# Narrow part of a matmul gradient transposed, with new phase lengths and shared rounding

## The chip, the cores and the metric

The kernel runs on one core of one Trainium2 chip. The metric is the device time of one execution in microseconds (us). Engines are named as in the profile: PE is the matmul engine, PEld its weight loads, DVE the vector engine, ACT the scalar engine, POOL and SP the engines that here mostly issue DMAs. L123 is line 123 of the kernel that the view belongs to, so line numbers differ between kernels. The granted clock is the share of PE's full clock that the profile says PE was given.

## The reference

```python
# input: 16 x 512 x 1024 float32, grad_output: 16 x 512 x 768 float32
grad_weight = np.einsum('bmk,bmn->kn', input, grad_output)     # 1024 x 768
```

Batch and rows together are 8192 rows, taken in 64 **slices** of 128 rows. Each slice gives X (128 x 1024) and G (128 x 768), and the result is the sum over all slices of X transposed times G.

## The kernel before: the parts that matter

All 1024 x 768 outputs would take twelve PSUM tiles of 128x512 float32 (**banks**), and the kernel's pool holds eight, so the slices are worked in **phases**. In each phase, the wide part (512 of the 768 columns of G) takes eight banks, one for each 128 rows of the output. Then the narrow part (256 columns) follows. At the end of a pass a bank is added to an accumulator in SBUF.

```python
PHASES = [2, 4, 6, 10, 14, 18, 10]
...
if not last:                                   # wide: slice by slice, 8 banks
    for i, s in enumerate(slices[:-1]):
        for k in range(KS):
            nc.tensor.matmul(banks[k], xblk[s](k), gwide[s], start=(i == 0), stop=False)
for k in range(KS):
    if last:                                   # last phase: one bank after the other,
        bank = psum.tile([P, NA], f32, name="bank")     # each over all its slices
        for i, s in enumerate(slices[:-1]):
            nc.tensor.matmul(bank, xblk[s](k), gwide[s], start=(i == 0), stop=False)
    ...
# narrow_group: X block as weights, 256 columns of G stream
for i, s in enumerate(slices):
    nc.tensor.matmul(dst, xblk[s](k), gnarrow[s][:, c0:c1], ...)
```

Slices 0 and 1 come as float32 and are rounded to bf16 on DVE and ACT. All others come through a POOL queue that rounds on the way. Eleven warm-up matmuls run while the first data load.

## Time and profile before

| | before |
|---|---|
| time, median (range) | 177.36 us (177.28 to 177.38) |
| span of the profiled execution | 175.6 us |
| PE busy | 171.2 us, 97% of the span |
| DMA engines | about full until 144 us |
| first real matmul, start of the last matmul | 5.43 us, 172.57 us |

The gap of 1.76 us between time and span lies outside the profile. "Busy" does not mean "at its peak" for PE, because matmuls are pipelined and overlap in the record. The distance between two starts is the measure, and it comes from the chain of waits in order of time. The groups by shape give counts and the length of one instruction. Columns: line, engine, operation, output and inputs, count, then busy us and mean ns of one, then idle us before them.

```profile
L144 PE MATMUL bank<-gt,xt 128*128 128x512 bf16 x367 | 81.5, 379 | 0.5
L123 PE MATMUL bank<-gt,xt 128*128 128x256 bf16 x486 | 54.0, 273 | 0.0
L123 PEld LDWEIGHTS <-xt 128*128 128x128 bf16 x506 | 48.7, 98 | 6.8
```

A matmul of 512 columns is on record for 379 ns, though they start 215.8 ns apart. Weight loads of 98 ns lie beside matmuls. Some matmul records are missing (367 of 376 in the first line), so idle time below is computed from the first and last start and the instruction count, not by summing gaps.

### The profile page before, as it was taken

How to read it: one execution, taken by the hardware profiler on the slowest of the kernel's cores; microseconds unless marked ns; L12 is line 12 of the kernel's file. 1: busy time of each engine (PE TensorE's matmuls, PEld its weight loads, DVE VectorE, ACT ScalarE, POOL GpSimd, SP SyncE). 2: the span in 40 equal slices, each digit the busy share in tenths (PEclk: the TensorE clock that was granted, in tenths of full speed). 3: DMA queues.
4: the chain of work that ended last, by engine and by line, in shares of the span. 5: the costliest groups of instructions: out<-in, count | busy, mean ns of one | idle time of the engine just before them, and what ended most of it. 6: DMA issues, size and time to landing. Idle time of an engine off the chain costs nothing.

```text
span 175.6 us, 2484 instructions
## 1 busy us (share of the span) xinstructions
PE 171.2 (97%) x1033; PEld 101.7 (58%) x1045; DVE 54.2 (31%) x93; ACT 8.0 (5%) x15; POOL 66.6 (38%) x129
## 2 busy tenths in 40 slices
PE   8999999999999999999999999999999999999993
PEld 3364844764446864444488744444458886444783
DVE  0662990970008530000381300000047112333332
ACT  2451300000000000000000000000000000000000
POOL 7444434444444444444444444444364100000000
PEclk9999999999999999999999999999999999999999
DMA  5999999999999999999999999999999990333432
GB/s 196 288 207 209 208 208 209 209 208 209 207 208 207 209 209 210 208 209 207 209 207 209 208 210 208 209 206 208 208 210 208 209 169 0 119 119 119 144 126 92
DMA packets 21595, 33.45 MB, mean 190 GB/s; under 512 B 2385, under 2 KB 12497, under 8 KB 21585
## 3 DMA queue, kind: packets, MB, share of 16 engines
q0 software_dynamic: 18128, 28.58, 89.1%
q1 hardware_dynamic: 3168, 3.67, 6.0%
q10 hardware_dynamic: 288, 1.05, 1.5%
q8 instruction: 8, 0.13, 0.3%
q14 instruction: 3, 0.02, 0.0%
HBM read 58.72 MB, written 3.15 MB: 352 GB/s over the span
## 4 chain that ended last, share of the span: by engine, by line
PE 81%; DMA 15%; POOL 1%; issue 1%; DVE 0%; POOLq 0%
PE bank L144 38%; PE bank L123 29%; DMA xt<-in_input_dram 15%; PE bank L149 9%; PE bank L153 5%; POOL gt L101 1%; POOL gn L88 0%; POOL xt L102 0%; DVE acc L119 0%; POOLq L199 0%
## 5 line engine op out<-in xcount | busy, mean ns | idle before, releaser
L144 PE MATMUL bank<-gt,xt 128*128 128x512 bf16 x367 | 81.5, 379 | 0.5
L119 DVE TENSOR_TENSOR acc<-bank,acc 128x512 f32<-128x512 f32 (+2 forms) x69 | 41.8, 646 | 107.6 <-PE bank L153 82.1
L144 PEld LDWEIGHTS <-xt 128*128 128x128 bf16 x376 | 36.8, 98 | 43.3 <-DMA xt<-in_input_dram 0.2
L123 PE MATMUL bank<-gt,xt 128*128 128x256 bf16 (+1 forms) x506 | 55.2, 270 | 0.0
L123 PEld LDWEIGHTS <-xt 128*128 128x128 bf16 x506 | 48.7, 98 | 6.8
L102 POOL DMA_DIRECT2D xt<-in_input_dram x62 | 33.0, 532 | 38.7 <-DMA xt<-in_input_dram 33.8
L101 POOL DMA_DIRECT2D gt<-in_grad_output_dram x62 | 32.9, 531 | 30.7 <-DMA gt<-in_grad_output_dram 28.8
L149 PE MATMUL bank<-gt,xt 128*128 128x512 bf16 x70 | 16.7, 379 | 0.1
L153 PE MATMUL bank<-gt,xt 128*128 128x512 bf16 x47 | 12.4, 379 | 0.2 <-DMA xt<-in_input_dram 0.2
L149 PEld LDWEIGHTS <-xt 128*128 128x128 bf16 x72 | 7.1, 98 | 8.3
L153 PEld LDWEIGHTS <-xt 128*128 128x128 bf16 x48 | 4.5, 97 | 6.4 <-DMA xt<-in_input_dram 1.2
L113 DVE COPY acc<-bank 128x512 f32<-128x512 f32 x10 | 6.2, 683 | 5.7 <-PE bank L153 5.7
L68 PE MATMUL bank<-const-bfloat16-1.0 128*128 128x512 bf16 x11 | 4.9, 630 | 0.8 <-PEq L199 0.8
L115 ACT COPY acc<-bank 128x512 f32<-128x512 f32 x10 | 5.3, 597 | 6.1 <-PE bank L153 5.7
L119 DVE TENSOR_TENSOR acc<-acc,acc 128x512 f32<-128x512 f32 x8 | 5.0, 680 | 0.0
L68 PEld LDWEIGHTS <-const-bfloat16-1.0 128*128 128x128 bf16 x11 | 1.5, 143 | 3.2 <-issue 3.2
L73 DVE CAST g<-gf 128x512 bf16<-128x512 f32 x2 | 0.9, 426 | 5.6 <-DMA gf<-in_grad_output_dram 5.6
L144 PE MATMUL bank<-g,x 128*128 128x512 bf16 x8 | 2.1, 415 | 0.0
L123 PE MATMUL bank<-gn,x 128*128 128x256 bf16 x16 | 1.9, 273 | 0.0
L153 PE MATMUL bank<-g,x 128*128 128x512 bf16 x8 | 1.9, 379 | 0.0
L123 PEld LDWEIGHTS <-x 128*128 128x128 bf16 x16 | 1.6, 98 | 0.4
L144 PEld LDWEIGHTS <-x 128*128 128x128 bf16 x8 | 0.8, 108 | 1.6 <-DVE x L79 0.7
(9 smaller groups left out, 5.7 us busy)
## 6 DMA issues: line engine op xcount, KB each, us to landing
xt<-in_input_dram POOLq DMA_DIRECT2D x62, 256.0 KB, 8.5
gt<-in_grad_output_dram POOLq DMA_DIRECT2D x62, 192.0 KB, 8.5
out_dram<-acc SPq DMA_DIRECT2D x13, 128.0 KB, 1.7
out_dram<-acc SPq DMA_DIRECT2D x5, 256.0 KB, 2.0
xf<-in_input_dram ACTq DMA_DIRECT2D x2, 512.0 KB, 4.9
gf<-in_grad_output_dram SPq DMA_DIRECT2D x2, 256.0 KB, 4.6
gn<-in_grad_output_dram POOLq DMA_DIRECT2D x1, 128.0 KB, 6.1
out_dram<-acc SPq DMA_DIRECT2D x2, 64.0 KB, 1.6
```

Source lines behind the costliest of these rows:

```text
L68: nc.tensor.matmul(wps, ones, ones_wide, start=(i == 0), stop=(i == WARMUP - 1))
L73: nc.vector.tensor_copy(out=gt, in_=gf[s])
L101: nc.gpsimd.dma_start(out=gt, in_=G[s * P : (s + 1) * P, :])
L102: nc.gpsimd.dma_start(out=xt, in_=X[s * P : (s + 1) * P, :])
L113: nc.vector.tensor_copy(out=dst, in_=src)
L115: nc.scalar.copy(out=dst, in_=src)
L119: nc.vector.tensor_add(out=dst, in0=src, in1=dst)
L123: nc.tensor.matmul(dst, xblk[s](k), gnarrow[s][:, c0:c1], start=(i == 0), stop=(i == len(slices) - 1),)
L144: nc.tensor.matmul(banks[k], xblk[s](k), gwide[s], start=(i == 0), stop=False)
L149: nc.tensor.matmul(bank, xblk[s](k), gwide[s], start=(i == 0), stop=False)
L153: nc.tensor.matmul(bank, xblk[s](k), gwide[s], start=False, stop=True)
```

## The change

The intent: stream X in pieces of 512 columns for the narrow part too, with 128 columns of G as weights. The narrow result then comes out transposed. At the end DVE turns it in 32x32 blocks, and the store puts the blocks in place. Taking even and odd columns of G as two weight sets lets neighbouring columns meet again in the turned tile, so that stored runs are 64 floats and not 32. The phases become shorter at the start, and the last one is longer. The last phase also changes its order: it begins with the narrow pass, slice by slice, and the wide blocks follow one by one. Its last output block is cut in three, so that the last add and store are 128 columns wide, as they were before. The core of the diff (cut):

```diff
-PHASES = [2, 4, 6, 10, 14, 18, 10]
+PHASES = [2, 3, 4, 5, 8, 10, 18, 14]
...
-        nc.vector.tensor_copy(out=gt, in_=gf[s])          # G whole on DVE
-        ... quarters of X on DVE and ACT in turn
+        for dst, src in ((gt, gf[s]), (xt, xf[s])):       # both in 256-column pieces
+            for i in range(0, dst.shape[1], 2 * QX):
+                nc.vector.tensor_copy(out=dst[:, i : i + QX], in_=src[:, i : i + QX])
+                nc.scalar.copy(out=dst[:, i + QX : i + 2 * QX], in_=src[:, i + QX : i + 2 * QX])
...
+            t, h = groups[j]                              # t: even or odd, h: half of X
             nc.tensor.matmul(
-                dst, xblk[s](k), gnarrow[s][:, c0:c1], ...
+                banks[j],
+                gnarrow[s].rearrange("p (r t) -> p t r", t=NT)[:, t],
+                xs[s][:, h * NA : (h + 1) * NA], ...
...
+    def add_and_turn(t, h, dst, src):
+        add_out(dst, src)
+        nc.vector.transpose(out=turned[:, h * hb : (h + 1) * hb, :, t],
+                            in_=dst.rearrange("p (b r) -> p b r", r=SQ))
...
+        # last phase: narrow first, slice by slice; then the wide blocks one by one
+        narrow_pass(slices, add_and_turn, streamed=True)
+        store_turned()                                    # four stores, 256-byte runs
         for k in range(KS):
+            pieces = [(0, NA)] if k < KS - 1 else [(0, 256), (256, 384), (384, NA)]
```

More of the change, by code (lines that the diff above doesn't have):

```diff
@@ L35 @@
     NB = N - NA
+    NT = NB // P
+    KH = K // NA
     assert sum(PHASES) == S and PHASES[0] == HW
@@ L45 @@
     psum = ctx.enter_context(tc.tile_pool(name="psum", bufs=8, space=bass.MemoryType.PSUM))
-    acc = accp.tile([P, KS, N], f32, name="acc")
-    acc1 = accp.tile([P, KS, NA], f32, name="acc1")
-    xblk = [None] * S
+    acc = accp.tile([P, KS, NA], f32, name="acc")
+    acct = accp.tile([P, NT, K], f32, name="acct")
+    spare = accp.tile([P, KS, NA], f32, name="spare")
+    xs = [None] * S
     gwide = [None] * S
@@ L72 @@
         gt = head.tile([P, NA], bf16, name=f"g{s}")
-        nc.vector.tensor_copy(out=gt, in_=gf[s])
-        xq = []
-        for i in range(K // QX):
-            xt = head.tile([P, QX], bf16, name=f"x{s}_{i}")
-            src = xf[s][:, i * QX : (i + 1) * QX]
-            if i % 2 == 0:
-                nc.vector.tensor_copy(out=xt, in_=src)
-            else:
-                nc.scalar.copy(out=xt, in_=src)
-            xq.append(xt)
-        xblk[s] = lambda k, xq=xq: xq[k // 2][:, (k % 2) * P : (k % 2 + 1) * P]
+        xt = head.tile([P, K], bf16, name=f"x{s}")
+        for dst, src in ((gt, gf[s]), (xt, xf[s])):
+            for i in range(0, dst.shape[1], 2 * QX):
+                nc.vector.tensor_copy(out=dst[:, i : i + QX], in_=src[:, i : i + QX])
+                nc.scalar.copy(out=dst[:, i + QX : i + 2 * QX], in_=src[:, i + QX : i + 2 * QX])
+        xs[s] = xt
         gwide[s] = gt[:, :]
@@ L102, in load_upto @@
             nc.gpsimd.dma_start(out=xt, in_=X[s * P : (s + 1) * P, :])
-            xblk[s] = lambda k, xt=xt: xt[:, k * P : (k + 1) * P]
+            xs[s] = xt
             gwide[s] = gt[:, 0:NA]
@@ L119, in add_out, with wide_mm @@
         nc.vector.tensor_add(out=dst, in0=src, in1=dst)
-    def narrow_group(dst, k, slices, c0, c1):
-        for i, s in enumerate(slices):
-            nc.tensor.matmul(
-                dst,
-                xblk[s](k),
-                gnarrow[s][:, c0:c1],
-                start=(i == 0),
-                stop=(i == len(slices) - 1),
+    SQ = 32
+    def wide_mm(bank, k, s, start, stop, c0=0, c1=NA):
+        nc.tensor.matmul(
+            bank, xs[s][:, k * P : (k + 1) * P], gwide[s][:, c0:c1], start=start, stop=stop
+        )
@@ new lines, in wide_pass, with narrow_pass, mm @@
+    def wide_pass(slices, evacuate):
+        banks = [psum.tile([P, NA], f32, name="bank") for _ in range(KS)]
+        for s in slices:
+            for k in range(KS):
+                wide_mm(banks[k], k, s, s == slices[0], s == slices[-1])
+                if s == slices[-1]:
+                    evacuate(k, banks[k])
+    def narrow_pass(slices, evacuate, streamed):
+        groups = [(t, h) for t in range(NT) for h in range(KH)]
+        banks = [psum.tile([P, NA], f32, name="bank") for _ in groups]
+        def mm(j, s):
+            t, h = groups[j]
+            nc.tensor.matmul(
+                banks[j],
+                gnarrow[s].rearrange("p (r t) -> p t r", t=NT)[:, t],
+                xs[s][:, h * NA : (h + 1) * NA],
+                start=(s == slices[0]),
+                stop=(s == slices[-1]),
+            )
+        if streamed:
+            for s in slices[:-1]:
+                for j in range(len(groups)):
+                    mm(j, s)
+        for j, (t, h) in enumerate(groups):
+            for s in slices[-1:] if streamed else slices:
+                mm(j, s)
+            evacuate(t, h, acct[:, t, h * NA : (h + 1) * NA], banks[j])
@@ new lines, with store_turned @@
+    turned = spare.rearrange("p a b -> p (a b)")[:, 0 : NT * K].rearrange(
+        "p (b r t) -> p b r t", t=NT, r=SQ
+    )
+    def add_and_turn(t, h, dst, src):
+        add_out(dst, src)
+        hb = NA // SQ
+        nc.vector.transpose(
+            out=turned[:, h * hb : (h + 1) * hb, :, t],
+            in_=dst.rearrange("p (b r) -> p b r", r=SQ),
+        )
+    def store_turned():
+        rows = out.rearrange("(b r) n -> r b n", r=SQ)
+        for a in range(P // SQ):
+            c = NA + a * NT * SQ
+            nc.scalar.dma_start(
+                out=rows[:, :, c : c + NT * SQ],
+                in_=turned[a * SQ : (a + 1) * SQ].rearrange("p b r t -> p b (r t)"),
@@ L140, with evacuate_wide @@
         if not last:
-            banks = [psum.tile([P, NA], f32, name="bank") for _ in range(KS)]
-            for i, s in enumerate(slices[:-1]):
+            def evacuate_wide(k, bank):
+                if ph == 0:
+                    copy_out(acc[:, k, :], bank)
+                elif ph == 1:
+                    copy_out(spare[:, k, :], bank)
+                else:
+                    add_out(acc[:, k, :], bank)
+            wide_pass(slices, evacuate_wide)
+            narrow_pass(
+                slices,
+                lambda t, h, dst, src: (copy_out if ph == 0 else add_out)(dst, src),
+                streamed=False,
+            )
@@ L143 @@
+            if ph == 1:
                 for k in range(KS):
-                    nc.tensor.matmul(banks[k], xblk[s](k), gwide[s], start=(i == 0), stop=False)
+                    add_out(acc[:, k, :], spare[:, k, :])
+            continue
+        narrow_pass(slices, add_and_turn, streamed=True)
+        store_turned()
         for k in range(KS):
-            if last:
-                bank = psum.tile([P, NA], f32, name="bank")
-                for i, s in enumerate(slices[:-1]):
-                    nc.tensor.matmul(bank, xblk[s](k), gwide[s], start=(i == 0), stop=False)
-            else:
-                bank = banks[k]
@@ L152 @@
-            s = slices[-1]
-            nc.tensor.matmul(bank, xblk[s](k), gwide[s], start=False, stop=True)
-            if ph == 0:
-                copy_out(acc[:, k, 0:NA], bank)
-            elif ph == 1:
-                copy_out(acc1[:, k, :], bank)
-            else:
-                add_out(acc[:, k, 0:NA], bank)
-            if last:
-                W = NB if k < 3 else NA
-                for c in range(0, NA, W):
-                    nc.sync.dma_start(out=OUT[:, k, c : c + W], in_=acc[:, k, c : c + W])
@@ L166 @@
-        if not last:
-            for k in range(0, KS, 2):
-                bank = psum.tile([P, 2, NB], f32, name="bank")
-                for j in range(2):
-                    narrow_group(bank[:, j, :], k + j, slices, 0, NB)
-                dst = acc[:, k : k + 2, NA:N]
-                (copy_out if ph == 0 else add_out)(dst, bank)
-        else:
-            for k in range(KS):
-                pieces = [(0, NB)] if k < KS - 1 else [(0, NB // 2), (NB // 2, NB)]
-                for c0, c1 in pieces:
-                    bank = psum.tile([P, NA], f32, name="bank")
-                    narrow_group(bank[:, 0 : c1 - c0], k, slices, c0, c1)
-                    dst = acc[:, k, NA + c0 : NA + c1]
-                    add_out(dst, bank[:, 0 : c1 - c0])
-                    nc.sync.dma_start(out=OUT[:, k, NA + c0 : NA + c1], in_=dst)
@@ L182 @@
-        if ph == 1:
-            for k in range(KS):
-                add_out(acc[:, k, 0:NA], acc1[:, k, :])
+            pieces = [(0, NA)] if k < KS - 1 else [(0, 256), (256, 384), (384, NA)]
+            for c0, c1 in pieces:
+                bank = psum.tile([P, NA], f32, name="bank")[:, 0 : c1 - c0]
+                for s in slices:
+                    wide_mm(bank, k, s, s == slices[0], s == slices[-1], c0, c1)
+                add_out(acc[:, k, c0:c1], bank)
+                W = NB if k < 6 else c1 - c0
+                for c in range(c0, c1, W):
+                    nc.sync.dma_start(out=OUT[:, k, c : c + W], in_=acc[:, k, c : c + W])
```

## The prediction

> **What bounds the kernel now.** I read the page first: busy shares, the 40 slices, the chain that ended last.
>
> ```profile
> PE 171.2 (97%) x1033; PEld 101.7 (58%) x1045; DVE 54.2 (31%) x93; ACT 8.0 (5%) x15; POOL 66.6 (38%) x129
> ...
> PE   8999999999999999999999999999999999999993
> ...
> PEclk9999999999999999999999999999999999999999
> DMA  5999999999999999999999999999999990333432
> ...
> PE 81%; DMA 15%; POOL 1%; issue 1%; DVE 0%; POOLq 0%
> ```
>
> The matmul engine is busy from end to end at the full clock. The DMA engines are nearly as full until about 144 us, so both limits lie close together. Busy does not mean at its peak, so I took the matmul pace from the chain in order of time:
>
> ```profile
> 20.89 9.49 DMA xt<-in_input_dram
> 30.38 0.05 issue
> 30.42 1.90 PE bank L153 x8
> 32.32 5.24 PE bank L123 x48
> ...
> 39.56 10.74 PE bank L144 x49
> 50.30 0.05 issue
> ...
> 131.04 15.72 PE bank L123 x144
> ...
> 164.03 8.77 PE bank L123 x90
> 172.80 0.02 issue
> 172.83 0.29 DVE acc L119
> ```
>
> From 30.42 us on, the chain is matmuls without a gap. The 49 matmuls of 512 columns and the 0.05 us "issue" piece are 50 issues in 10.79 us: 0.2158 us each. The 256-column ones take 15.72/144 = 0.1092 us. The last 90 are 70 of 256 columns (7.64 us) and 20 of 128 columns, which leaves 1.13/20 = 0.056 us each. Before 30.42 us the chain runs over loads. The timeline shows the first real matmul at 5.43 us, where the last warm-up matmul also ends. From 5.43 to 30.42 are 24.99 us, and the work in them is 88 x 0.2158 + 48 x 0.1092 = 24.23 us. So all the idle time of the matmul engine is **0.76 us**: about 0.24 us at the first matmuls (8 take 2.13 us where the next 8 take 1.89) and about 0.52 us waiting for slices 5 and 11 (the weight loads of L153 wait for input tiles twice, 1.2 us in all, part of it behind running matmuls).
>
> The end: last add over at 173.12 us, span 175.6 us, so 2.5 us for the last store. Time per run is 177.36, thus 1.76 us more than the span; I keep that constant.
>
> **What the Trainium skill says.** "TensorE: Matmul & The Clock Gate", section "Wait — 56ns, not 53.3ns?": a warm matmul starts N/2.4 GHz plus about 2.5 ns after the one before it, 215.7 ns at N = 512. The trace agrees at all three widths (215.8, 109.2, about 56 ns). So the column count sets the cost and a narrow matmul only pays the 2.5 ns more often. The same page, "Weight-path perf modes — Fast Weight Load (FWL) and DoubleRow", lists for fast weight loads "4 chunks of 32 columns, packed or strided", column steps up to 1,024 elements; the even or odd columns have step 2. No weight load of the kernel before is strided, so its trace cannot confirm it. "VectorE: DVE Perf Modes", "The three transpose paths": the vector engine's transpose works in 32x32 blocks only, which is why the new store must put blocks in place. "DMA: Bandwidth & Descriptors", "Specifications", asks for at least 512 B per transfer for line rate; the new store moves runs of 64 floats, 256 B.
>
> **The change part by part.** The order of the built program's instructions shows 807 matmuls (11 warm-ups) in place of 1055.
>
> *Narrow product.* Out: 502 matmuls of 256 columns and 20 of 128. In: 64 x 4 = 256 of 512 columns, G as weights and X streaming. Before: 502 x 0.1092 + 20 x 0.056 = 55.94 us. After: 256 x 0.2158 = 55.24. Gain 0.70 us.
>
> *Wide product.* 512 of 512 columns before. After, the last output block (14 slices) is cut in 256 + 128 + 128: 14 x (0.1092 + 2 x 0.056) = 3.10 us for 14 x 0.2158 = 3.02. Loss 0.08 us. Together the matmul work falls from 166.43 to 165.81 us, **-0.62 us**. Half as many weight loads in the narrow part are worth nothing: they overlap matmuls (at 128 columns two successive matmuls lie 56 ns apart although a load lasts 98 ns).
>
> *Rounding at the start.* Both engines now share G and X. A 256-column cast takes 0.30 us on DVE, 0.40 on ACT. X's first quarter could be ready at about 5.2 us, not 5.34, but the warm-up holds the matmul engine until 5.43. **0.**
>
> *Phase lengths.* I lay the new phases out by 12 x 0.2158 = 2.59 us per slice. First phase: 5.43 + 0.24 + 24 x 0.2158 = 10.85. Then phase ends 18.62 (3 slices), 28.98 (4), 41.9 (5), 62.6 (8), 88.5 (10), 135.1 (18). Landings are read from the load queue, whose waits end every 2.2 us: slice 4 at 14.24, slice 8 at 24.0, slice 13 at 35.1. Wanted: slice 4 at 10.85 + 16 x 0.2158 = 14.30 (just there), slice 8 at 18.62 + 24 x 0.2158 = 23.80 (late by 0.2), slice 13 at 36 (early). So about 0.2 us of waiting in place of 0.52: **-0.32 us**. In the last phase the streamed narrow pass wants slice 63 at 135.3 + 13 x 0.863 = 146.5 us; the last load was issued at 136.55 with a median 8.5 us to landing: 145.1, so 1.4 us to spare.
>
> *PSUM banks.* The short phases press on DVE. Its pace back to back comes from these rows:
>
> ```profile
> 22.66 3.69 DVE L119 TENSOR_TENSOR acc<-acc,acc 128x512 f32<-128x512 f32 x6
> 30.85 7.44 DVE L119 TENSOR_TENSOR acc<-bank,acc 128x512 f32<-128x512 f32 x12 [4.50 <-PE bank L153]
> ```
>
> (7.44 - 0.68)/11 = 0.614 us from PSUM and (3.69 - 0.68)/5 = 0.60 from SBUF. In the 3-slice phase DVE's narrow adds end about 19.7, the eight adds of the spare accumulator 24.5, the eight wide adds of the 4-slice phase 29.4, its four narrow adds 31.9. The next phase starts at 29.2 and in plain order would want its eighth bank at 29.2 + 7 x 0.2158 = 30.7: a stall of 1.2 us. But the built order puts matmuls of its second slice between: the bank freed last is written 15th, at 29.2 + 14 x 0.2158 = 32.2, and the first recycled narrow bank 6th, at 30.3 against 30.15. It just fits: **0**, with 0.15 to 0.3 us of margin.
>
> *End.* The four adds and four transposes of the last phase (estimate 0.6 us each, as for an add of the same size, so about 5 us on DVE) end near 152, while the wide blocks run until 171.7. The 1 MB of transposed output goes out in 4096 runs of 256 B. The stores before: 3168 packets on that queue for 6.0% of 16 x 175.6 us, 53 ns each, so 4096 x 53/16 = 13.6 us if they were no faster; there are 20 us, at a DMA share of about 0.3. Last piece: 128 columns, a 0.29 us add and 64 KB, as before. **0.**
>
> Sum: 177.36 - 0.62 - 0.32 = **176.4 us**.
>
> **The rivals.** *A strided weight load is slow.* Twice 98 ns stays behind a matmul of 216 ns; only beyond that does it show, 256 times (at four times the load, 256 x 0.18 = 45 us). For it: nothing measured here is strided. Against: the margin. I give it 2%. *DVE becomes the wait in phases 3 to 5.* Adds 0.02 us slower would use up the margin and cost about 0.3 us; if reordering failed, 1.2 us at that phase and less at the next: 177 to 178. *The small-run store reaches the tail.* The third and fourth wait for semaphores of other stores, so the fourth starts only near 162 us; if 256 KB of small runs took 10 us, the last stores would land later: +0.5 to 2 us, 177 to 178.5. *Loads late in the last phase.* If the load stream slips by over 1.4 us: up to +1 us. *No effect at all*: the matmul work is almost the same column count, so the phase gain could vanish in a later wait for loads: 177.0.
>
> **Range and chances.** Every rival but the last adds to 176.4, so the range leans up: 175.8 to 177.8. Two per cent are 3.5 us. The gain cannot be that large: all idle time is 0.76 us and all per-matmul overhead in the narrow part 0.7 us. A loss of that size needs the slow weight load or two rivals at once. Faster 0.01, same 0.96, slower 0.03.
>
> **What would show it.** Right: 256 narrow matmuls 0.216 us apart; strided weight loads near 98 ns and never followed by idle matmul time; matmul idle of 0.3 to 0.5 us after 5.43; last matmul near 171.7; packets under 512 B up by some 4096, all landed before 170; last-store stretch still 2.5 us. Wrong: matmuls waiting for DVE between 29 and 45 us; narrow spacing above 0.216; a chain that ends in a store of the transposed tile; a wait for input tiles after 135 us.

## The result, and the profile after

The changed kernel takes **176.23 us** (median of 4, 176.15 to 176.43) against 177.34 us for the kernel before, measured beside it. The ratio is 0.9939, 95% interval 0.9922 to 0.9957. Ratios here are the mean time of one kernel's fast runs over that of the other's of the same rounds, so they are not quite the ratios of the medians. A second measurement on another chip gave 0.9939 again (the control below). By the threshold of 2% this is "same"; it is a real gain of 1.1 us all the same.

From the page of the changed kernel, the busy times, the DMA packets and the chain by engine:

```profile
PE 169.8 (97%) x792; PEld 78.1 (45%) x807; DVE 62.7 (36%) x106; ACT 8.7 (5%) x17; POOL 66.9 (38%) x129
...
DMA packets 25176, 33.42 MB, mean 192 GB/s; under 512 B 6480, under 2 KB 16592, under 8 KB 25168
...
PE 94%; DMA 3%; issue 1%; DVE 0%; ACTq 0%
```

PE's share of the chain went from 81% to 94%, and that of DMA from 15% to 3%. In the kernel before the chain left PE for loads until 30 us; now it leaves it only until slice 1 is there. The chain in order of time (start, us, what) shows where:

```profile
1.18 5.72 DMA xf<-in_input_dram
...
7.28 1.90 PE bank L124 x8
9.18 1.73 PE bank L145 x8
...
122.97 10.74 PE bank L145 x49
133.71 0.05 issue
...
166.14 5.43 PE bank L124 x52
...
171.59 0.29 DVE acc L119
```

From 7.28 us, the first matmul of slice 1, to the end there is no wait for data or for a bank. L145 are the narrow matmuls, and (10.74 + 0.05)/50 = 0.2158 us is their distance, as for wide ones. By shape:

```profile
L145 PE MATMUL bank<-xt,gt 128*128 128x512 bf16 x244 | 54.3, 379 | 0.2
L145 PEld LDWEIGHTS <-gt 128*128 128x128 bf16 x248 | 24.2, 98 | 29.3
L171 DVE STREAM_TRANSPOSE spare<-acct 128x512 f32<-128x512 f32 x4 | 2.6, 684 | 0.0
```

The weight loads with step 2 last 98 ns, as those with step 1 did. A transpose of 128x512 float32 lasts 684 ns, as long as an add of the same size.

**Where the time went.** The first real matmul starts at 5.23 us in this profile but at 5.44 us in the control's profile of the same kernel (5.43 before): in one execution the warm-up ran at the full clock a little earlier. So I compare the kernel before with the control. The last matmul starts at 172.57 and 171.53 us, 1.04 us earlier. From the first start to the last, the kernel before takes 167.13 us, of which 166.37 are work at the measured distances; 0.76 us are idle. The control takes 166.08 us with 165.75 of work; 0.33 us are idle. So 0.62 us come from work, which is counts times measured distances, and 0.43 us from idle time. Not all of that idle time is waiting. In both profiles the first two real matmuls start 0.41 us after one another and the next one 0.26 us (before) or 0.31 us (control) later, where 0.216 is the distance afterwards; the clock record of the kernel before shows the full clock only from 5.93 us on. These slow starts cost 0.24 us before and 0.29 us in the control. What is left, the waiting for loads, is 0.52 us before and 0.04 us in the control: it has all but gone. The stretch from the end of the last add to the end of the span is 2.48 us before and 2.47 us after, unchanged.

### The profile page after: what moved, and what is told of

The parts are those of the page before. It is cut to its first block, busy times and chain, and to the rows that moved or that the text cites. A ratio compares the mean times of both kernels' runs of the same rounds, so it can differ in the third digit from the quotient of the medians.

```text
span 174.3 us, 2019 instructions
## 1 busy us (share of the span) xinstructions
PE 169.8 (97%) x792; PEld 78.1 (45%) x807; DVE 62.7 (36%) x106; ACT 8.7 (5%) x17; POOL 66.9 (38%) x129
## 2 busy tenths in 40 slices
DMA packets 25176, 33.42 MB, mean 192 GB/s; under 512 B 6480, under 2 KB 16592, under 8 KB 25168
## 4 chain that ended last, share of the span: by engine, by line
PE 94%; DMA 3%; issue 1%; DVE 0%; ACTq 0%
PE bank L124 62%; PE bank L145 32%; DMA xf<-in_input_dram 3%; ACTq L65 0%; DVE x L81 0%; DVE acc L119 0%
## 5 line engine op out<-in xcount | busy, mean ns | idle before, releaser
L124 PE MATMUL bank<-gt,xt 128*128 128x512 bf16 (+2 forms) x513 | 107.7, 367 | 0.6
L124 PEld LDWEIGHTS <-xt 128*128 128x128 bf16 x524 | 50.2, 98 | 57.2 <-DMA xt<-in_input_dram 0.2
L119 DVE TENSOR_TENSOR acc<-bank,acc 128x512 f32<-128x512 f32 (+2 forms) x50 | 30.2, 665 | 74.1 <-PE bank L124 74.1
L145 PE MATMUL bank<-xt,gt 128*128 128x512 bf16 x244 | 54.3, 379 | 0.2
L145 PEld LDWEIGHTS <-gt 128*128 128x128 bf16 x248 | 24.2, 98 | 29.3
L119 DVE TENSOR_TENSOR acct<-bank,acct 128x512 f32<-128x512 f32 x28 | 18.2, 688 | 25.8 <-PE bank L145 25.8
L119 DVE TENSOR_TENSOR acc<-spare,acc 128x512 f32<-128x512 f32 x8 | 4.9, 691 | 0.0
L113 DVE COPY acc<-bank 128x512 f32<-128x512 f32 x4 | 2.5, 684 | 0.3 <-PE bank L124 0.3
L171 DVE STREAM_TRANSPOSE spare<-acct 128x512 f32<-128x512 f32 x4 | 2.6, 684 | 0.0
L115 ACT COPY acc<-bank 128x512 f32<-128x512 f32 x4 | 2.1, 602 | 0.3 <-PE bank L124 0.3
L145 PE MATMUL bank<-x,gn 128*128 128x512 bf16 x8 | 1.9, 379 | 0.0
```

Source lines behind the costliest of these rows:

```text
L113: nc.vector.tensor_copy(out=dst, in_=src)
L115: nc.scalar.copy(out=dst, in_=src)
L119: nc.vector.tensor_add(out=dst, in0=src, in1=dst)
L124: nc.tensor.matmul(bank, xs[s][:, k * P : (k + 1) * P], gwide[s][:, c0:c1], start=start, stop=stop)
L145: nc.tensor.matmul(banks[j], gnarrow[s].rearrange("p (r t) -> p t r", t=NT)[:, t], xs[s][:, h * NA : (h + 1) * NA], start=(s == slices[0]) ...
L171: nc.vector.transpose(out=turned[:, h * hb : (h + 1) * hb, :, t], in_=dst.rearrange("p (b r) -> p b r", r=SQ),)
```

## The experiments

My theory after the result: the gain is two separate things, the fixed cost of a matmul start saved 256 times in the narrow part (0.6 us), and the waits for slices 5 and 11 that the new phases avoid (0.4 to 0.5 us). The rounding and the rest are hidden. Rivals: that one of the parts carries all of it, that the choice of stationary operand or the strided loads matter, that DVE or the store have slack to burn. Eleven runs were made, the control among them, all with correct results.

### Control: the changed kernel again

No edit.

> The changed kernel unchanged, as a control: 176.2 us, ratio 0.994.

Measured: 176.31 us (176.06 to 176.60), ratio 0.9939, interval 0.9926 to 0.9951. As expected.

### The transposed narrow part alone

```diff
-PHASES = [2, 3, 4, 5, 8, 10, 18, 14]          # in the changed kernel
+PHASES = [2, 4, 6, 10, 14, 18, 10]
-        (new rounding)
+        nc.vector.tensor_copy(out=gt, in_=gf[s])          # and X in quarters in turn
```

> The changed kernel with the old phase lengths 2,4,6,10,14,18,10 and the old rounding: the transposed narrow part alone. My theory (0.6 us less matmul work, waits for slices 5 and 11 as before): 176.7 to 176.8 us, ratio 0.9966. Rival (all the gain is in the phases): 177.35. Weight loads of the strided columns 98 ns.

Measured: 176.96 us, ratio 0.998, interval 0.9967 to 0.9992, so a gain of 0.35 us with an interval of 0.14 to 0.59. The expected ratio of 0.9966 lies just outside. The chain shows the waits of the kernel before come back at the same places:

```profile
...
21.05 9.36 DMA xt<-in_input_dram
30.41 0.05 issue
30.46 1.90 PE bank L124 x8
```

The end is tied to the landing of slice 11 at 30.4 us, which a faster PE does not move. Idle time after the first matmul is 0.86 us here, 0.10 more than before. What the narrow matmuls save ahead of that landing turns into waiting, but that is little: only 24 of the 256 lie there, worth 0.06 us. From the first matmul of slice 11 to the start of the last matmul this kernel takes 141.59 us and the kernel before 142.15, so 0.56 us, nearly the whole gain of the narrow part, is there. In this profile 0.11 us of it is lost again behind the last add (2.59 us to the end of the span, for 2.48). The waits of the old phases stay, so the rest of the gain needs the new ones.

### Old phases, new rounding

```diff
-PHASES = [2, 3, 4, 5, 8, 10, 18, 14]          # in the changed kernel
+PHASES = [2, 4, 6, 10, 14, 18, 10]
```

> The changed kernel with the old phase lengths 2,4,6,10,14,18,10; the rounding stays new. My theory: it differs from the transposed narrow part alone only by the rounding, which is worth at most 0.12 us: 176.6 to 176.75. Rival (the rounding carries the start): 176.4 or less, and the narrow part alone above 176.8.

Measured: 176.91 us, ratio 0.9975, interval 0.9963 to 0.9988. That is above the expected 176.6 to 176.75 us, but it agrees with the run before it, so the rounding gives nothing to see. In its profile slice 11 starts at 30.18 us, in that of the run before at 30.46 us; from there both take 141.59 us to the last matmul, so with the old phases it is this landing that sets the end. Against the control's 0.9939, the new phases are worth 0.0036 x 177.3 = 0.64 us in the changed kernel, with an uncertainty of some 0.3 us.

### Old rounding

```diff
-        (new rounding, in the changed kernel)
+        nc.vector.tensor_copy(out=gt, in_=gf[s])          # and X in quarters in turn
```

> The changed kernel with the old rounding (G whole on the vector engine, quarters of X alternate). Theory of the prediction: 0, so 176.2. What the two traces suggest: slice 1 starts at about 7.40 and not 7.28 us, so 176.35. Rival (the start is set by the landing of slice 1's X alone, 6.9 us): no change of the start of slice 1 beyond 0.1 us.

Measured: 176.28 us, ratio 0.9932, interval 0.992 to 0.9945, not different from the changed kernel. In its profile the first real matmul starts at 5.44 us and slice 1 at 7.44 us; in the control, with the new rounding, they start at 5.44 and 7.47 us. The rounding is worth nothing that shows, as the prediction said; what I had read into the two traces was the difference between two executions.

### X streamed in pieces of 256 columns

```diff
+            for c in range(0, NA, 256):      # in all phases but the last
+                for s in slices:
+                    nc.tensor.matmul(banks[j][:, c : c + 256], <same weights>,
+                                     xs[s][:, h * NA + c : h * NA + c + 256], ...)
```

> The changed kernel with X streamed in pieces of 256 columns in the narrow passes of all phases but the last: 400 matmuls of 256 columns in place of 200 of 512, all else the same. My theory (the gain of the narrow part is only the fixed 2.6 ns per pair of matmuls): +200 x 0.0026 = 0.52 us, so 176.75 us, the narrow matmuls 0.1092 us apart. Rival (the gain comes from which operand is stationary, or from fewer weight loads): within 0.1 us of 176.23.

Measured: 176.86 us, ratio 0.9972, interval 0.996 to 0.9985. Against the control that is 0.0033 x 177.3 = +0.58 us, with an uncertainty of some 0.3 us, where the count said +0.52. The orientation is the same as in the changed kernel; the number of matmuls differs, and with it the number of weight loads, since each matmul has its own. So the gain in the narrow part is a fixed cost for each load and matmul together; that G is stationary is only the means to have 512 columns to stream. That the matmul and not the load costs the 2.6 ns is not shown by this run. What speaks for it is that loads of 98 ns do not slow matmuls of 128 columns, which start 56 ns apart.

### Front of the new phases in the kernel before

```diff
-PHASES = [2, 4, 6, 10, 14, 18, 10]            # in the kernel before
+PHASES = [2, 3, 4, 5, 8, 14, 18, 10]
```

> The kernel before with only the phase lengths changed, to 2,3,4,5,8,14,18,10: the short front of the new list, but the old last phase of 10. My theory (the phases are worth the 0.3 to 0.5 us of waiting for slices 5 and 11, and nothing else): about 176.9 us, ratio 0.997, narrow matmuls still 0.109 us apart, matmul idle after 7.4 us down from about 0.5 to under 0.25 us. Rival (the gain is all in the narrow matmuls): 177.35, same idle time moved elsewhere. Second rival (the vector engine becomes the wait in the short phases): above 177.8.

Measured: 177.14 us, ratio 0.9986, interval 0.9973 to 1.0, a gain of 0.25 us that is only just clear of nothing. In its profile slices 5 and 11 are no longer waited for, and 0.1 us of idle time are left after the first matmul, 0.08 of them a wait for slice 8 at 24.0 us; but that first matmul started only at 5.76 us, because the float32 loads landed later in this execution. The spans say more than the times. In all five executions of this run 2.06 to 2.16 us of the time lie outside the span, where the kernel before, in the same rounds, has 1.73 to 1.82. The mean span is 175.06 us for 175.60 before: 0.54 us less, about the 0.45 expected. So the phases do save the waits here, and some 0.3 us of it is lost outside the profile, for a reason that the record does not show.

### All new phases in the kernel before

```diff
-PHASES = [2, 4, 6, 10, 14, 18, 10]            # in the kernel before
+PHASES = [2, 3, 4, 5, 8, 10, 18, 14]
```

> The kernel before with the whole new phase list 2,3,4,5,8,10,18,14 and nothing else. Theory: its last phase takes all slices for the first output block at once and so wants slice 63 about 3 us after the phase starts at 135.7 us, but slice 63 lands near 145: about 6 us of idle matmul time there, 183 to 184 us, slower than before. Only the narrow pass that goes slice by slice lets the last phase have 14 slices. Rival (phase lengths are neutral on their own): 177.0 to 177.4.

Measured: 185.96 us, ratio 1.0478, interval 1.0459 to 1.0497: **slower by 4.8%**. The timeline of PE in the last phase (start, us, engine, line, operation, count, idle before it and what ended it):

```profile
138.75 0.39 PE L149 MATMUL bank<-gt,xt 128*128 128x512 bf16 x1 [0.45 <-DMA xt<-in_input_dram]
140.96 0.39 PE L149 MATMUL bank<-gt,xt 128*128 128x512 bf16 x1 [1.82 <-DMA xt<-in_input_dram]
143.16 0.61 PE L149 MATMUL bank<-gt,xt 128*128 128x512 bf16 x1 [1.81 <-DMA xt<-in_input_dram]
145.37 0.61 PE L153 MATMUL bank<-gt,xt 128*128 128x512 bf16 x1 [1.59 <-DMA xt<-in_input_dram]
```

The first output block of the last phase runs over all 14 slices at once, and the last four have not landed. The waits are 5.7 us. The rest was not expected: the granted clock falls to 0.50 from 142.4 to 149.2 us (a mean of 0.60 from 146 to 150 us), and the 14 matmuls from 145.37 to 150.27 us take 4.9 in place of 3.0 us. The lesson is about the pair of changes: a last phase of 14 slices is only possible because the changed kernel begins it with a narrow pass that uses one slice every 4 x 0.2158 = 0.863 us. There it wants slice 63 at 146.3 us; here that slice was there at 145.4.

### Narrow pass at the end of the last phase

```diff
-        narrow_pass(slices, add_and_turn, streamed=True)      # ahead of the wide blocks
-        store_turned()
         for k in range(KS):
             ...
+        narrow_pass(slices, add_and_turn, streamed=True)      # behind them
+        store_turned()
```

> The changed kernel with the last phase's narrow pass, transposes and store moved behind its wide blocks. Theory: the wide blocks then want slice 63 near 138 us while it lands near 145 (about 6 to 7 us idle), and the last group's add, two transposes and the store of 256 B runs stand at the end, 2.4 + 3.4 to 5 us in place of 0.3 + 2.4: about 185 to 187 us in all. Rival (the transposes and the store are cheap wherever they stand, and the order is free): below 178.

Measured: 195.00 us, ratio 1.0984. Slower as expected, by more than expected. PE idles 6.0 us on the same late slices, and the granted clock is 0.50 from 140.8 to 151.0 us, so the last matmul starts at 181.44 us. What follows it takes 12.5 us in place of 3.0. The timeline of the end:

```profile
182.42 1.30 DVE L171 STREAM_TRANSPOSE spare<-acct 128x512 f32<-128x512 f32 x2
183.63 1.25 DVE L119 TENSOR_TENSOR acct<-bank,acct 128x512 f32<-128x512 f32 x2
184.81 1.28 DVE L171 STREAM_TRANSPOSE spare<-acct 128x512 f32<-128x512 f32 x2
186.18 3.46 ACTq L180 DMA_DIRECT2D out_dram<-spare x4
```

I had counted the last group only; but the streamed pass ends its four groups together, so four adds and four transposes (4.9 us), 3.5 us to issue the four stores and a median 4.2 us to their landing follow one another. That is what the changed kernel hides behind 24 us of wide matmuls.

### Contiguous halves as weights, runs of 128 B

```diff
-                gnarrow[s].rearrange("p (r t) -> p t r", t=NT)[:, t],
+                gnarrow[s][:, t * P : (t + 1) * P],
-        four stores of 32 x 32 x 64 floats
+        eight stores of 32 x 32 x 32 floats
```

> The changed kernel with contiguous halves of the narrow G columns as weights in place of even and odd ones: weight loads of step 1, and the transposed output in 8192 runs of 128 B, eight stores. Theory (a strided weight load costs nothing, and the store hides): weight loads still 98 ns, narrow matmuls 0.216 us apart, 176.2 to 176.4 us. Rival (strided loads cost something): below 176.0. Rival (small runs reach the tail): the stores of 128 B runs land after 170 us and the time is above 176.8.

Measured: 176.56 us, ratio 0.995, interval 0.9936 to 0.9963. Weight loads of step 1 also last 98 ns. The strided loads cost nothing, so the rival that they do has fallen. The time is 0.25 us above the changed kernel's and above the expected 176.2 to 176.4 us, which the intervals do not separate surely. All its small stores were issued by 162.7 us and landed within 3.7 us, so by 166.5 us, well ahead of the end. Its stretch from the last matmul's start to the end of the span is 3.26 us for 3.01 in the control. The traces settle why: in both the last store lands at 173.63 us, but SP then still goes through five of its closing waits, about 0.06 us each, where the control has one. The small stores themselves are not late.

### Last output block left whole

```diff
-            pieces = [(0, NA)] if k < KS - 1 else [(0, 256), (256, 384), (384, NA)]
+            pieces = [(0, NA)]
```

> The changed kernel with the last output block left whole (14 matmuls of 512 columns, one add, one store). Theory: matmul work 0.08 us less, but the last add takes 0.69 in place of 0.29 us and the last store is 256 KB (2.0 us to landing in place of 1.6): 176.23 - 0.08 + 0.4 + 0.4 = 176.95. Rival (the cut is not worth it): 176.2 or less.

Measured: 177.18 us, ratio 0.9989, interval 0.9976 to 1.0002: +0.9 us against the changed kernel, a little more than worked out. The last add lasts 0.69 us in place of 0.29, and from its end to the end of the span are 3.06 us in place of 2.47. So cutting the last block is worth over ten times the 0.08 us of matmul starts that it costs.

### More work on DVE at the short phases

```diff
                 for k in range(KS):
                     add_out(acc[:, k, :], spare[:, k, :])
+                for k in range(4):                            # of no use, on purpose
+                    nc.vector.tensor_copy(out=spare[:, k, :], in_=acc[:, k, :])
```

> The changed kernel with four extra vector copies of 128x512 (2.4 us) behind the eight adds of the spare accumulator. Theory (the vector engine just keeps up between 24 and 32 us, margin 0.15 to 0.3 us): matmuls wait for the vector engine near 28 us and the time rises by 1.5 to 2.2 us, to about 178. Rival (there is ample slack, the matmul engine does not see it): within 0.2 us of 176.2.

Measured: 177.16 us, ratio 0.999, interval 0.9976 to 1.0004, so 0.9 us more than the changed kernel. The rival of ample slack has fallen; the size I expected was wrong. The timeline:

```profile
24.35 1.43 DVE L212 COPY spare<-acc 128x512 f32<-128x512 f32 x4
25.69 4.87 DVE L119 TENSOR_TENSOR acc<-bank,acc 128x512 f32<-128x512 f32 x8
26.43 3.62 PE L145 MATMUL bank<-xt,gt 128*128 128x512 bf16 x16 [0.71 <-DVE acc L119]
```

The four copies from SBUF to SBUF delay the wide adds by 25.69 - 24.35 = 1.34 us, not 2.4: a float32 copy between SBUF tiles lasts 0.42 us, an add 0.68. The Trainium skill says as much ("VectorE: DVE Perf Modes", section "The perf-mode tier table (the rule you actually need)": 2x for a float32 copy in SBUF, 1x for `tensor_tensor`), and I had not looked it up for this. The first narrow matmul then waits for the first wide add to free its bank. It starts at 26.43 us where 25.55 would follow without a gap (25.34 + 0.2158), so 0.88 us of the 1.34 reach PE. The slack there is about 0.5 us, and the changed kernel's own trace agrees: that add ends at 24.90 us and the bank is written at 25.41.

## Why the prediction was right or wrong

**The bound** was read right: two resources close together, PE at its pace and the loads just ahead of it, with 0.76 us of idle time and no more. Only 0.52 us of that was waiting that phase lengths could win; the 0.24 us at the first matmuls are slow starts, and they stayed.

**Narrow and wide work, -0.62 us:** right. (The 1055 matmuls of the prediction are a slip: its own counts and the page's weight loads give 1045. No sum uses it.) The distances are 0.2158 us for the new narrow matmuls and 0.1092 us where they were cut again, and cutting 200 of them gave +0.58 us for +0.52 counted, with an uncertainty of 0.3.

**Phase lengths, -0.32 us:** right in mechanism, too small in size. Waiting for loads fell from 0.52 to 0.04 us. The step that failed is "slice 8 at 24.0 ... late by 0.2": landings were read from the kernel before and taken to stay where they were. In the load queue a row waits for the load issued eight rows earlier, so that these rows tell of slice 8, first in the kernel before:

```profile
23.44 0.53 POOL L101 DMA_DIRECT2D gt<-in_grad_output_dram  x1 [2.03 <-DMA gt<-in_grad_output_dram]
24.05 0.53 POOL L102 DMA_DIRECT2D xt<-in_input_dram  x1
```

and then in the changed one:

```profile
23.10 0.53 POOL L102 DMA_DIRECT2D xt<-in_input_dram  x1 [0.71 <-DMA xt<-in_input_dram]
25.50 0.53 POOL L101 DMA_DIRECT2D gt<-in_grad_output_dram  x1 [1.86 <-DMA gt<-in_grad_output_dram]
```

Before, one long wait (2.03 us) is for G of slice 8, and X of slice 8 follows; the row at 24.05 us has no wait of its own, and the semaphore record of the trace dates that landing at 23.76 us. In the changed kernel the long wait (1.86 us) comes one load later, for G of slice 9. Its X of slice 8 lands at 22.82 us, 0.9 us earlier, and PE, which wants it at 23.5, does not stop. That this wait would move was not foreseen, so it was luck that slice 8 cost nothing.

All 13 traces fall in these two groups: X of slice 8 lands at 23.6 to 24.0 us where narrow matmuls have 256 columns (the kernel before, both runs of new phases in it, and the pieces of 256), and at 22.8 to 23.2 us in the other nine. The pieces of 256 differ from the changed kernel in nothing else, so the number of narrow matmuls and loads moves it. How, the DMA records suggest: in each trace the late load is the first to land after the end of the first transfer of the queue that the page calls "q8 instruction" (16 KB, about 0.9 us long). That transfer starts at 20.6 to 21.1 us in the first group and at 22.9 to 23.5 us in the second. That it makes the load late is argued from the order alone; no run tests it.

By time, the experiment with the old phases gives 0.64 us for the new ones with an uncertainty of 0.3. In the kernel before, the front of the phases gives 0.25 us, and 0.54 us by the span.

**Rounding, 0:** right, by the experiment with the old rounding. The argument (the warm-up ends when the data come) held in the control and failed in the first profile of the changed kernel, where PE started 0.2 us earlier and then waited longer for slice 1.

**PSUM banks, 0:** right. The bank named as the first recycled was free at 29.68 and written at 29.95 us, the last at 31.48 and 31.89: margins of 0.27 and 0.41 us for the 0.15 to 0.3 predicted. The tightest place, the first narrow matmul at 25.41 us, was not in the prediction. It too had room, 0.5 us.

**End, 0:** right; 2.47 us for 2.48. Packets under 512 B rose from 2385 to 6480, by 4095. The four small-run stores were issued from 151.7 to 163.0 us and took 3.1 to 4.9 us to land, so all were down by 168. The prediction's 53 ns for a packet, from a queue that carries loads of G too, did not come into play.

**The rivals:** the strided weight load is refuted at 98 ns. DVE does not make PE wait; with 1.34 us more on it, it did, by 0.88 us. The small-run store does not reach the tail in place; out of place, the adds, transposes and stores together make what follows the last matmul's start 9.5 us longer. Loads were not late in the last phase: slice 63 landed at 145.1 us and was wanted at 146.3, so 1.1 us to spare (1.4 predicted). The sum of -0.94 us was measured as -1.1 us.

## What to carry to other kernels

When PE is dense, count matmul starts: a fixed 2.6 ns for each pair of 256-column matmuls made into one of 512 is all that reorienting the product brought here, and it can be worked out in advance from the distances in the chain. Phase lengths belong to the order of loops that consumes the slices: the same list that won half a microsecond with a slice-by-slice pass at the head of the last phase lost 8.6 us without it. A landing read in one kernel's trace need not hold in the next: here slice 8 came 0.9 us earlier although the loads and their order are the same. And look at the span beside the time, because what lies outside it was not the same for every kernel (1.8 us, or 2.0 to 2.1).

## What the Trainium skill lacked or had wrong

- "TensorE: Matmul & The Clock Gate", section "Back-to-back issue gap", gives for streams of load and matmul about 131 ns per matmul at N = 512 and about 81 ns at N = 128. Every stream here ran, at the full clock, at 215.8 ns and, at 128 columns, about 56 ns, each matmul with its own weight load. The figures in "Wait — 56ns, not 53.3ns?" fit.
- The same page, "Weight-path perf modes — Fast Weight Load (FWL) and DoubleRow", allows strided columns but gives no duration. Here step 2 and step 1 both take 98 ns.
- The same page's table "Why this matters for your kernels" asks for no PE-idle gaps over about 3 us, and its passage on micro-idles gives no size. In the run of all new phases in the kernel before, four gaps of 0.45 to 1.82 us with single matmuls between them went with a granted clock of 0.50 from 142.4 to 149.2 us.
- "VectorE: DVE Perf Modes", section "The three transpose paths", has 311 ns for 128x128 bf16 only; "Vector Engine (DVE) Microarchitecture Reference" has a rate, one element per cycle and lane, but no time. A float32 transpose of 128x512 in 32x32 blocks with an output step of 2 took 684 ns, the same as an add of that size.
- "DMA: Bandwidth & Descriptors", section "Specifications", asks for 512 B for line rate. Further down the page gives an overhead per packet of 256 B, but no time of a store in such runs on this chip. Here a store of 256 KB in runs of 256 B took a median 3.4 us to land beside other stores, one of 128 KB in runs of 128 B 2.7 us, and issuing four of the former back to back took 3.5 us.
- No page speaks of a kernel's loads being late beside the transfers that bring its own instructions; "Runtime: NRT & Kernel Launch", section "Instruction fetch mechanics", treats only the engine that fetches. In all 13 traces the first load to land after the first such transfer (16 KB, about 0.9 us) was 1.0 to 1.6 us later than the pace of the loads around it. That the transfer is the cause is not tested.
